# A two-layer hybrid block: the first memory columns from whole fp32 operands, reciprocal roots on GpSimd, post-norm products on VectorE, memory on ScalarE's queue

## The chip, the core and the metric

The kernel runs on one core of a Trainium2 chip. The metric is the device time of one execution in microseconds (us); lower is better. Engines are named as in the profile: PE (TensorE), PEld (its weight loads), ACT (ScalarE), DVE (VectorE), POOL (GpSimd), SP (SyncE, which issues most transfers). An "x" after a group gives its number of instructions.

## What is computed

Two layers over 256 tokens of width 1024, with a memory of 256 rows of width 1024. In each layer the normalised tokens are projected to 18 sections of 512 columns and to 5 x 1024 gate columns; five branches (stick-breaking attention, mLSTM, retention, attention to the memory, a gated MLP over tokens) are each projected up to 1024 columns, gated and summed; an out projection, a norm of its rows and the residual close the layer.

```python
def rms_norm(x, g):
    return x * lax.rsqrt(jnp.mean(x * x, axis=-1, keepdims=True) + EPS) * g

def hybrid_layer(x, mem, ...):
    proj = rms_norm(x, norm_pre) @ w_in
    ...                                             # y_sb, y_ml, y_gm, y_rt
    mkv = rms_norm(mem, mem_norm) @ w_mem_kv        # [256, 1024]: keys, values
    mem_k, mem_v = jnp.split(mkv, 2, axis=-1)
    y_xa = memory_attention(xa_q, mem_k, mem_v)
    up = einsum('bsnw,nwd->bsnd', ys, w_up)
    merged = sum(sigmoid(gates) * up, axis=2)
    return x + rms_norm(merged @ w_out, norm_post)
```

## The kernel before, in words

**Weights.** All weights stream through the core once as *halves* of 128 x 1024 fp32 (512 KB), in the order in which they are used: for each layer two chunks of memory keys (`mk`), two of memory values (`mv`), the 18 sections, gates and up projections, the out projection. A chunk is two halves. `load` (L141) issues a half's transfer on SP into one of four `raw` buffers. `split` (L155, L156) makes two fp32r tiles of it: ACT casts `whi`, DVE subtracts to get `wlo`; then it issues the load four halves on. Where a product is wanted, PE adds three fp32r matmuls, whi x hi, whi x lo and wlo x hi (L226 to L228 in `mm_proj`, L247 to L250 in `half_vproj`), the other operand being split in the same way. Plain fp32 operands are used in the branches (for example L497, L689); one such matmul shows as two records of PE.

**Order.** `step` runs one half: the split two halves on, the half's matmuls, an evacuation of PSUM, and then some units of other work from a queue. The order of instructions on each engine comes from a scheduler that works with estimated times; only SP's order, and at the very end ACT's, DVE's and POOL's too, is that of the program text.

**Start.** Five matmuls on zeros (L1102) come first. `memory` (1 MB, transposed, 8 blocks of 256 columns) and the first halves are loaded by SP in turn. `mem_split` (L329, L330) multiplies each block by the norm's gain and splits it: ACT makes `mh`, DVE makes `ml`. The first two halves give 256 memory columns (`psk`). `mem_rows` squares and sums the memory on POOL (L191 to L197), takes column sums on PE, and reciprocal roots by `rsqrt`; the rows are scaled after the projection. `x_norm_units` then norms the tokens, transposes them on PE and splits them into `hh` and `hl` (L356, L357). When the four memory chunks are through, `posb` (the positions) is loaded and `rope_tables` (L289 to L310) makes the tables of sines on DVE and ACT, ahead of the first layer.

**Reciprocal roots.** `rsqrt` is a bit trick with three Newton steps on DVE: nine small instructions for one column (L102, L103, L111, and three times L115 and L116), more for two or eight. It is used in the norms of the memory, of the tokens (`row_rsqrt`), of the branches' heads and of the gated MLP.

**End of layer 0.** The out projection leaves its result in four PSUM banks `pout`. ACT squares them (L215) and copies them to `og` (L1039), POOL multiplies by the gain (L1040); for the first 128 tokens ACT scales and POOL adds to the residual (L1048, L1049), for the others DVE does both in one (L1046). At the same time PE goes on with the memory chunks of layer 1, whose halves need ACT and DVE for `split`.

**End of layer 1.** `tail` does the same in a fixed order: products of the first 128 tokens on DVE (L1072), of the others on POOL (L1070), residuals on DVE (L1060) and once on POOL (L1083), and four output transfers.

Of the kernel before, what the change touches and what calls it, by code (L numbers as in the profile page):

```python
# [9 lines left out]
F32 = mybir.dt.float32  # L10
# [72 lines left out]
def hybrid_kernel(ctx: ExitStack, tc: tile.TileContext, x, mem, wpl, wmv, pos, vec, row, post, gmw, cst, out):  # L83
# [13 lines left out]
    def rsqrt(v, n, tag):  # L97
        """1/sqrt(v) for v > 0, [128, n]."""
        ti = tp.tile([128, n], I32, tag=tag + "i", name=tag + "i", bufs=1)
        y = tp.tile([128, n], F32, tag=tag + "y", name=tag + "y", bufs=2)  # L100
        t = tp.tile([128, n], F32, tag=tag + "t", name=tag + "t", bufs=1)
        dve.tensor_scalar(ti, v.bitcast(I32), 1, None, op0=ALU.logical_shift_right)  # L102
        dve.tensor_scalar(y[:].bitcast(I32), ti, -1.0, 1597463007.0, op0=ALU.mult, op1=ALU.add)  # L103
        if n > 2:
            for _ in range(3):
                dve.tensor_tensor(t, y, y, op=ALU.mult)
                dve.scalar_tensor_tensor(t, t, -0.5, v, op0=ALU.mult, op1=ALU.mult)
                dve.scalar_tensor_tensor(y, t, 1.5, y, op0=ALU.add, op1=ALU.mult)
            return y
        m = tp.tile([128, n], F32, tag=tag + "m", name=tag + "m", bufs=1)  # L110
        dve.tensor_scalar(m, v, -0.5, None, op0=ALU.mult)  # L111
        for _ in range(3):
            for j in range(n):
                c = slice(j, j + 1)
                dve.scalar_tensor_tensor(t[:, c], y[:, c], m[:, c], y[:, c], op0=ALU.mult, op1=ALU.mult)  # L115
            dve.scalar_tensor_tensor(y, t, 1.5, y, op0=ALU.add, op1=ALU.mult)  # L116
        return y

    # ------------------------------------------------------------------ weights
# [12 lines left out]
    def load(h, pieces=1):  # L132
        """half h of the weights; returns one transfer per piece, so that others can come between them."""
# [10 lines left out]
    def split(hi_, parts=1, between=None):  # L144
        """hi + lo = w exactly, each with a 12-bit significand."""
# [17 lines left out]
    # ------------------------------------------------------------------ constants  # L163
# [11 lines left out]
    state = {}  # L175

# [3 lines left out]
    # ------------------------------------------------------------------ norms  # L180
    def bcast_col(ps, cols):
        """cols [128 tokens, 2] (one column per token block) -> ps [128, T], the same on all partitions."""
        for tb in range(2):
            pe.transpose(ps[:, tb * 128:(tb + 1) * 128], cols(tb).to_broadcast([128, 128]), ident)

    def mem_rows():
        """1/rms of the memory rows: a column per token block, and broadcast over the partitions."""
        src = state["mem"]
        s0 = tp.tile([128, 512], F32, tag="t2", name="sq0", bufs=5)
        f = lambda i: src[:, 2 * i:2 * i + 2, :].rearrange("p a b -> p (a b)")  # L190
        pool.tensor_tensor(s0, f(0), f(0), op=ALU.mult)  # L191
        for i in range(1, 4):
            s1 = tp.tile([128, 512], F32, tag="t2", name="sq1", bufs=5)
            pool.tensor_tensor(s1, f(i), f(i), op=ALU.mult)
            pool.tensor_tensor(s0, s0, s1, op=ALU.add)
        acc = tp.tile([128, T], F32, tag="t2", name="acc", bufs=5)
        pool.tensor_tensor(acc, s0[:, 0:256], s0[:, 256:512], op=ALU.add)  # L197
# [32 lines left out]
    def half_proj(hi_, ps, xh, xl):  # L230
        """one 128-column block over all of D, into ps[:, s, :]."""
# [5 lines left out]
    def half_vproj(hi_, pss, xh, xl, n):  # L237
        """n columns, tokens on partitions, 4 of the 8 blocks of D; pss: one AP per token block."""
# [14 lines left out]
    # ------------------------------------------------------------------ work queue between weight halves  # L253
# [23 lines left out]
    def step(mm, evac=None, units=1):  # L277
        """one weight half: its matmuls, the split two halves on, the evacuation, then units of other work."""
# [8 lines left out]
    # ------------------------------------------------------------------ start  # L287
# [31 lines left out]

    def mem_split(l):  # L320
# [774 lines left out]
    with tc.manual_schedule(engines={mybir.EngineType.SP}):  # L1095
# [20 lines left out]
        for f in first[4:]:  # L1116
            f[0]()
# [110 lines left out]
```

## Time and profile before

| | |
|---|---|
| median of 3 runs | 943.66 us (942.91 to 944.35) |
| span of the profiled execution, first to last instruction | 942.9 us; no other time of this execution is recorded |
| PE busy | 922.1 us, 98% of the span, 7436 matmuls |
| DVE / ACT / POOL busy | 634.2 (67%) / 498.9 (53%) / 73.9 us (8%) |
| transfers | 165.07 MB, mean 175 GB/s |

A matmul's busy time runs from its start to its modelled end, and successive matmuls overlap, so PE's pace is read from the distance of their starts. The granted clock (PEclk) of a stretch is 1.00 at 2.4 GHz and 0.50 at 1.2 GHz.

### The profile page before, as it was taken

The numbers are of one execution on the slowest core, as the hardware profiler recorded it, in microseconds if no ns is written. First come the engines' busy times: TensorE is split into PE (matmuls) and PEld (weight loads), VectorE is DVE, ScalarE is ACT, GpSimd is POOL, SyncE is SP. The second block draws the span as 40 slices with busy tenths as digits, with TensorE's granted clock in tenths as the row PEclk, the third lists the DMA queues.
The fourth block names the chain that finished last, engine by engine and source line by source line (L and its number), as shares of the span: only waits on it lengthen the run. The fifth ranks groups of instructions, "written<-read, shape, count | busy, mean of one in ns | idle before, by whom it ended". The sixth has DMA issues, their size and how long they took to land.

```text
span 942.9 us, 18022 instructions
## 1 busy us (share of the span) xinstructions
PE 922.1 (98%) x7436; PEld 906.3 (96%) x7436; DVE 634.2 (67%) x1021; ACT 498.9 (53%) x701; POOL 73.9 (8%) x75
## 2 busy tenths in 40 slices
PE   7999999999999999999999999999999999999995
PEld 5999999999999999999889999999999999999994
DVE  6654558987785666555796444798877747755665
ACT  5664495544654544444667457754447455444452
POOL 4200010000040000000051000001000400000001
PEclk7999999999999999999999999999999999999998
DMA  7575545454455455555746554445444654555551
GB/s 257 172 251 183 181 150 165 137 189 143 155 173 193 158 171 177 182 181 188 250 146 225 196 181 157 150 164 162 157 152 152 200 181 154 165 193 184 181 188 59
DMA packets 45731, 165.07 MB, mean 175 GB/s; under 512 B 5200, under 2 KB 5328, under 8 KB 45520
## 3 DMA queue, kind: packets, MB, share of 16 engines
q1 hardware_dynamic: 45504, 163.66, 52.8%
q8 instruction: 58, 0.95, 0.4%
q10 hardware_dynamic: 144, 0.26, 0.1%
q14 instruction: 25, 0.20, 0.1%
HBM read 162.85 MB, written 1.05 MB: 174 GB/s over the span
## 4 chain that ended last, share of the span: by engine, by line
PE 94%; DVE 2%; DMA 1%; ACT 0%; issue 0%; POOL 0%; DVEq 0%; ACTq 0%
PE psp L228 19%; PE psp L227 19%; PE psp L226 19%; PE psu L227 4%; PE psu L226 4%; PE psu L228 4%; PE psp L247 3%; PE psp L250 3%; PE psp L249 3%; PE pout L1008 1%; PE pout L1006 1%; PE pout L1007 1%; PE psv L249 1%; PE psv L250 1%; PE psv L247 1%; PE pss L689 1%
## 5 line engine op out<-in xcount | busy, mean ns | idle before, releaser
L156 DVE TENSOR_TENSOR wlo<-raw,whi 128x1024 fp32r<-128x1024 f32 (+2 forms) x297 | 370.6, 1250 | 216.3 <-ACT whi L155 216.0
L155 ACT CAST whi<-raw 128x1024 fp32r<-128x1024 f32 (+2 forms) x297 | 310.3, 1047 | 358.8 <-PE psp L227 230.9
L226 PE MATMUL psp<-hh,whi 128*128 128x256 f32 x1536 | 433.6, 282 | 0.0
L227 PE MATMUL psp<-hl,whi 128*128 128x256 f32 x1536 | 433.3, 282 | 0.0
L228 PE MATMUL psp<-hh,wlo 128*128 128x256 f32 x1536 | 433.2, 282 | 0.0
L226 PEld LDWEIGHTS psp<-hh,whi 128*128 128x128 f32 x1536 | 289.5, 188 | 0.1
L227 PEld LDWEIGHTS psp<-hl,whi 128*128 128x128 f32 x1536 | 289.3, 188 | 0.1
L228 PEld LDWEIGHTS psp<-hh,wlo 128*128 128x128 f32 x1536 | 289.1, 188 | 0.2
L226 PE MATMUL psu<-yh,whi 128*128 128x256 f32 x320 | 90.3, 282 | 0.0
L227 PE MATMUL psu<-yl,whi 128*128 128x256 f32 x320 | 90.1, 282 | 0.0
L228 PE MATMUL psu<-yh,wlo 128*128 128x256 f32 x320 | 90.1, 281 | 0.0
L250 PE MATMUL psp<-whi,hl 128*128 128x256 f32 x224 | 63.1, 282 | 0.8 <-DVE hl L357 0.8
L247 PE MATMUL psp<-whi,hh 128*128 128x256 f32 x224 | 63.4, 283 | 0.0
L249 PE MATMUL psp<-wlo,hh 128*128 128x256 f32 x224 | 62.8, 281 | 0.0
L226 PEld LDWEIGHTS psu<-yh,whi 128*128 128x128 f32 x320 | 60.5, 189 | 0.0
L228 PEld LDWEIGHTS psu<-yh,wlo 128*128 128x128 f32 x320 | 60.5, 189 | 0.0
L227 PEld LDWEIGHTS psu<-yl,whi 128*128 128x128 f32 x320 | 60.3, 188 | 0.0
L250 PEld LDWEIGHTS psp<-whi,hl 128*128 128x128 f32 x224 | 42.3, 189 | 1.1 <-DVE hl L357 1.1
L247 PEld LDWEIGHTS psp<-whi,hh 128*128 128x128 f32 x224 | 42.4, 189 | 0.0
L249 PEld LDWEIGHTS psp<-wlo,hh 128*128 128x128 f32 x224 | 42.2, 188 | 0.0
L978 DVE SCALAR_TENSOR_TENSOR gate<-gate,psu 128x512 f32<-128x512 f32 x32 | 22.0, 687 | 13.0 <-PE psu L228 13.0
L1007 PE MATMUL pout<-wlo,mgh 128*128 128x512 f32 x64 | 25.2, 394 | 0.0
(294 smaller groups left out, 1086.2 us busy)
## 6 DMA issues: line engine op xcount, KB each, us to landing
raw<-in_wpl_dram SPq DMA_DIRECT2D x291, 512.0 KB, 3.7
raw<-in_wmv_dram SPq DMA_DIRECT2D x4, 528.0 KB, 4.5
rowb<-in_row_dram SPq DMA_DIRECT2D x2, 772.0 KB, 8.8
xn<-in_x_dram SPq DMA_DIRECT2D x2, 512.0 KB, 10.1
gpost<-in_post_dram SPq DMA_DIRECT2D x2, 512.0 KB, 4.8
memT<-in_mem_dram SPq DMA_DIRECT2D x1, 1024.0 KB, 4.8
cs<-in_cst_dram SPq DMA_DIRECT2D x1, 768.0 KB, 8.2
out_dram<-xn SPq DMA_DIRECT2D x3, 256.0 KB, 2.4
```

The costliest lines, as they stand in the source:

```text
L155: act.copy(hi[:, c], r[:, c])
L156: dve.tensor_tensor(lo[:, c], r[:, c], fview(hi[:, c]), op=ALU.subtract)
L226: pe.matmul(ps_ap, wh(k), xh(k), start=st, stop=False, skip_group_check=True)
L227: pe.matmul(ps_ap, wh(k), xl(k), start=False, stop=False, skip_group_check=True)
L228: pe.matmul(ps_ap, wl(k), xh(k), start=False, stop=last and k == nk - 1, skip_group_check=True)
L247: pe.matmul(ap, a, hi[:, kk * n:(kk + 1) * n], start=st and s == 0 and kk == 0, stop=False, skip_group_check=True)
L249: pe.matmul(ap, a, lo[:, kk * n:(kk + 1) * n], start=False, stop=False, skip_group_check=True)
L250: pe.matmul(ap, b, hi[:, kk * n:(kk + 1) * n], start=False, stop=s == 1 and kk == 3, skip_group_check=True)
L689: pe.matmul(ps[:, 0:256], k[:, h, 0:128], q[:, h, :], start=True, stop=False, skip_group_check=True)
L978: dve.scalar_tensor_tensor(g, g, 1.0, ps, op0=ALU.add, op1=ALU.mult)
L1006: pe.matmul(po[tb][i], a, hi[:, c], start=k == 0, stop=False)
L1007: pe.matmul(po[tb][i], a, lo[:, c], start=False, stop=False)
```

## The change

- **First memory columns.** `mem_gain` multiplies the memory by the gain on DVE into whole fp32 tiles, and `first_halves` multiplies the first two halves of the weights as loaded with these: 16 plain fp32 matmuls instead of two splits and 48 fp32r matmuls. The split memory, which the later chunks need, is still made (ACT `mh`; DVE `ml` from the product). The loads of halves 4 and 5 are issued behind these matmuls.
- **Transfers at the start.** The memory's four pieces of 256 KB are issued on ACT's queue; on SP come the gains first, then the pieces of the halves 0 and 1 in turn, halves 2 and 3, constants, tokens.
- **Sums of squares of the memory** go from POOL to ACT (squares) and DVE (three adds). The scaling of the first two `psk` banks comes after the second one.
- **Reciprocal roots.** `rsqrt` is one POOL instruction, a power with exponent -0.5, everywhere; the factor 1/D goes into the squares' scale.
- **Post norm.** In layer 0 and in `tail` the copies on ACT and products and sums on POOL are replaced: DVE multiplies PSUM by the row factor and the gain, then adds (layer 0), or multiplies and then adds with the row factor (`tail`).
- **Rope tables** are made from the queue during the projections of layer 0, behind the units that split memory keys and values.

```diff
     def rsqrt(v, n, tag):
         y = tp.tile([128, n], F32, tag=tag + "y", name=tag + "y", bufs=2)
-        dve.tensor_scalar(ti, v.bitcast(I32), 1, None, op0=ALU.logical_shift_right)
...
-            dve.scalar_tensor_tensor(y, t, 1.5, y, op0=ALU.add, op1=ALU.mult)
+        pool.tensor_tensor(y, v, mhalf[:, 0:n], op=ALU.pow)
         return y
+    def mem_squares():
+        src = state["mem"]
+        sq = [bp.tile([128, 4, T], F32, tag="z", name="msq", bufs=2) for _ in range(2)]
+        for i in range(2):
+            act.activation(sq[i], src[:, 4 * i:4 * i + 4, :], AF.Square, scale=1.0 / 32.0)
+        a, b = (t[:].rearrange("p a b -> p (a b)") for t in sq)
+        dve.tensor_tensor(a, a, b, op=ALU.add)
+        dve.tensor_tensor(a[:, 0:512], a[:, 0:512], a[:, 512:1024], op=ALU.add)
+        dve.tensor_tensor(a[:, 0:256], a[:, 0:256], a[:, 256:512], op=ALU.add)
+        state["msq"] = a
+    def first_halves(ps, xk):
+        w = [raws.pop(0), raws.pop(1)]
+        for k in range(KB):
+            for s in range(2):
+                pe.matmul(ps[:, s, :], w[s][:, k * 128:(k + 1) * 128], xk(k), start=k == 0 and s == 0,
+                          stop=k == KB - 1, skip_group_check=True)
+        count[0] = 2
+        for h in (4, 5):
+            for f in load(h):
+                f()
+    def mem_gain():
...
+        for k in range(KB):
+            dve.tensor_scalar(g[k // 4][:, k % 4, :], src[:, k, :], vcol(0, 8 + k), None, op0=ALU.mult)
+        for k in range(KB):
+            hi, lo = state["mh"][k // 4][:, k % 4, :], state["ml"][k // 4][:, k % 4, :]
+            act.activation(hi, src[:, k, :], AF.Copy, scale=vcol(0, 8 + k))
+            dve.tensor_tensor(lo, g[k // 4][:, k % 4, :], fview(hi), op=ALU.subtract)
+        return lambda k: g[k // 4][:, k % 4, :]
...
+            if l == 0 and c == 0:
+                first_halves(ps, state.pop("mg"))
+                mem_squares()
+                split(3)
+                late = [lambda ps=ps: evac(0, ps)]
+                continue
...
         queue.extend(mkv_split_units())
+        if l == 0:
+            queue.append(lambda: rope_tables(state.pop("pos")))
...
         def p1(tb):
-            og = pn[tb] = [tp.tile([128, 512], F32, tag="t2", name="og", bufs=5) for _ in range(2)]
             for i in range(2):
-                g = gpost[:, i * 512:(i + 1) * 512]
-                act.copy(og[i], po[tb][i])
-                pool.tensor_tensor(og[i], og[i], g, op=ALU.mult)
...
+                dve.scalar_tensor_tensor(og, po[tb][i], pn["r", tb], gpost[:, i * 512:(i + 1) * 512], op0=ALU.mult,
+                                         op1=ALU.mult)
+                dve.tensor_tensor(xs, xs, og, op=ALU.add)
...
                     sq = tp.tile([128, 512], F32, tag="t2", name="sq", bufs=5)
...
+                    act.activation(sq, po[tb][i], AF.Square, scale=1.0 / 32.0, accum_out=ss[:, j:j + 1])
+                    dve.tensor_tensor(og[tb][i], po[tb][i], gpost[:, c[i]], op=ALU.mult)
+                dve.scalar_tensor_tensor(v[:, tb:tb + 1], ss[:, 2 * tb:2 * tb + 1], EPS, ss[:, 2 * tb + 1:2 * tb + 2],
+                                         op0=ALU.add, op1=ALU.add)
+                r[tb] = rsqrt(v[:, tb:tb + 1], 1, f"n{tb}")
+                if tb == 0:
+                    last(0, 0, nc.sync)
+                    last(0, 1, nc.sync)
             last(1, 0, nc.scalar)
-            nc.sync.dma_start(out[:, 0, c[1]], xs(0, 1))
             last(1, 1, nc.sync)
...
+        for i in range(4):
+            nc.scalar.dma_start(state["mem"][:, 2 * i:2 * i + 2, :], mem[:, 2 * i:2 * i + 2, :])
         act.activation(warm, warm, AF.Exp)
...
         nc.sync.dma_start(vecs, vec)
...
+        for p in range(2):
+            first[0][p]()
+            first[1][p]()
         first[2][0]()
         first[3][0]()
         nc.sync.dma_start(cs[:, 0:C_RET], cst[:, 0:C_RET])
...
+        state["mg"] = mem_gain()
+        split(2)
         queue.append(mem_rows)
         queue.extend(x_norm_units(0))
-        mkv(0, [1, 0, 1, 2, 1, 1, 1, 1])
+        mkv(0, [1, 1, 2, 1, 2, 1])
```

## Rows read from the trace of the kernel before

**Rows 1.** The page's chain that ended last, shares of the span by engine.

```profile
PE 94%; DVE 2%; DMA 1%; ACT 0%; issue 0%; POOL 0%; DVEq 0%; ACTq 0%
```

**Rows 2.** Waits of PE over the span: total us, times, longest us.

```profile
PE psk L228 <- DVE wlo L156: 2.6, 2, 2.1
```

**Rows 3.** Windows at the start: busy of PE, PEld, DVE, ACT, POOL; PEclk, DMA share, GB/s.

```profile
4.00:6.00 2.00, 1.61 (x5) 1.00 (x3) 0.69 (x1) 0.56 (x1) 0.00 (x0) 1.00 0.75 162
6.00:8.00 2.00, 0.64 (x3) 0.44 (x4) 1.07 (x2) 1.10 (x3) 1.04 (x1) 1.00 1.00 363
...
20.00:22.00 2.00, 2.00 (x11) 2.00 (x11) 1.83 (x9) 1.42 (x6) 0.00 (x0) 0.50 0.80 270
```

**Rows 4.** Timeline of PE at the start: start us, us, instruction, idle before.

```profile
1.30 4.31 PE L1102 MATMUL pw<-wm 128*128 128x256 f32 x10 [1.30 <-POOL mlv L642]
...
6.95 0.38 PE L226 MATMUL psk<-mh,whi 128*128 128x256 f32 x1 [1.34 <-ACT mh L329]
...
22.95 0.27 PE L226 MATMUL psk<-mh,whi 128*128 128x256 f32 x1
```

**Rows 5.** Groups of instructions from 0 to 23 us: busy us, mean ns, idle before.

```profile
L330 DVE SCALAR_TENSOR_TENSOR ml<-memT,vecs,mh 128x256 fp32r<-128x256 f32 x8 | 9.0, 1186 | 1.7 <-ACT mh L329 1.7
...
L194 POOL TENSOR_TENSOR sq<-memT 128x512 f32<-128x512 f32 x3 | 3.9, 1321 | 1.1 <-DMA memT<-in_mem_dram 1.1
```

**Rows 6.** Timeline of PE at 117 us: two plain fp32 matmuls.

```profile
117.07 1.02 PE L497 MATMUL psz<-sb_q,sb_k 128*128 128x256 f32 x4
```

**Rows 7.** Groups over the span, forms kept apart: DVE, then POOL.

```profile
L156 DVE TENSOR_TENSOR wlo<-raw,whi 128x1024 fp32r<-128x1024 f32 x291 | 364.0, 1253 | 210.8 <-ACT whi L155 210.5
...
L811 DVE TENSOR_SCALAR xp<-xp,xs 128x256 f32<-128x256 f32 x16 | 4.9, 351 | 0.3
...
L1072 DVE TENSOR_TENSOR og<-pout,gpost 128x512 f32<-128x512 f32 x2 | 1.4, 692 | 3.2 <-ACT sq L1067 3.2
...
L873 POOL TENSOR_TENSOR gm_v<-gm_v,rowb 128x512 f32<-128x512 f32 x4 | 9.0, 2280 | 0.0
...
L197 POOL TENSOR_TENSOR acc<-sq 128x256 f32<-128x256 f32 x1 | 0.8, 795 | 0.1
```

**Rows 8.** The page's transfers of weight halves: KB each, median us to landing.

```profile
raw<-in_wpl_dram SPq DMA_DIRECT2D x291, 512.0 KB, 3.7
```

**Rows 9.** Timeline of DVE and PE from 48 to 52 us.

```profile
49.17 0.29 DVE L293 CAST pf<-posb 128x256 f32<-128x256 int32 x1 [3.36 <-DMA posb<-in_pos_dram]
...
49.91 0.39 PE L250 MATMUL psp<-whi,hl 128*128 128x256 f32 x1 [0.84 <-DVE hl L357]
...
51.74 0.39 PE L249 MATMUL psv<-wlo,hh 128*128 128x264 f32 x1 [0.60 <-DVE wlo L156]
```

**Rows 10.** Timeline of DVE and PE between the layers.

```profile
472.26 0.16 DVE L217 TENSOR_TENSOR rv<-ss 128x1 f32<-128x1 f32 x1 [1.17 <-ACT sq L215]
...
476.17 3.46 DVE L156 TENSOR_TENSOR wlo<-raw,whi 128x1024 fp32r<-128x1024 f32 x2
...
485.44 0.39 PE L228 MATMUL psk<-mh,wlo 128*128 128x256 f32 x1 [2.13 <-DVE wlo L156]
```

**Rows 11.** Windows between the layers, columns as in rows 3.

```profile
486.40:489.80 3.40, 3.40 (x19) 3.40 (x18) 3.33 (x8) 2.78 (x7) 0.79 (x1) 0.50 0.56 175
489.80:493.20 3.40, 3.40 (x30) 3.40 (x30) 3.40 (x8) 2.03 (x3) 2.05 (x2) 0.99 0.73 242
```

**Rows 12.** Timeline of the tail: DVE, ACT and SP's queue.

```profile
930.45 0.15 DVE L1078 SCALAR_TENSOR_TENSOR rv<-ss,rv 128x1 f32<-128x1 f32 x1
...
931.78 1.27 DVE L116 SCALAR_TENSOR_TENSOR n0y<-n0t,n0y 128x1 f32<-128x1 f32 x1
...
932.47 0.19 ACT L1067 ACTIVATION_READ_ACCUMULATOR sq<-pout 128x1 f32 x1
...
937.81 1.42 DVE L1060 SCALAR_TENSOR_TENSOR xn<-og,n1y,xn 128x512 f32<-128x512 f32 x2
...
939.25 0.33 SPq L1061 DMA_DIRECT2D out_dram<-xn  x1
```

More of the change, by code (lines that the diff above doesn't have):

```diff
@@ L175, in hybrid_kernel @@
     state = {}
+    mhalf = cp.tile([128, 8], F32, name="mhalf")
+    pool.memset(mhalf, -0.5)
     def vcol(l, o, n=1):
@@ L184, in bcast_col @@
             pe.transpose(ps[:, tb * 128:(tb + 1) * 128], cols(tb).to_broadcast([128, 128]), ident)
-    def mem_rows():
[L188 to L197, printed above, removed]
+    def mem_squares():
[8 more added lines that the diff above has]
+        state["msq"] = a
+    def mem_rows():
+        acc = state.pop("msq")
         ps = pz.tile([128, 512], F32, tag="sm", name="psn")
@@ L318, in mem_load @@
         nc.sync.dma_start(t, mem)
+    def mem_gain():
+        src = state["mem"]
+        g = [bp.tile([128, 4, T], F32, tag=n, name="mg", bufs=2) for n in "qk"]
+        state["mh"] = [bp.tile([128, 4, T], F32R, tag="yhi", name="mh", bufs=3) for _ in range(2)]
+        state["ml"] = [bp.tile([128, 4, T], F32R, tag="ylo", name="ml", bufs=3) for _ in range(2)]
+        for k in range(KB):
[5 more added lines that the diff above has]
+        return lambda k: g[k // 4][:, k % 4, :]
     def mem_split(l):
@@ L373, in mkv @@
                 ps = pz.tile([128, 2, T], F32, tag="sm", name="psk")
-            def evac():
-                dve.tensor_tensor(mk[2][:, 2 * c:2 * c + 2, :], ps,
-                                  rbm[:].unsqueeze(1).to_broadcast([128, 2, T]), op=ALU.mult)
-            for s in range(2):
-                step(lambda h: half_proj(h, ps, mh, ml), evac if s else None, units.pop(0))
+            if l == 0 and c == 0:
[4 more added lines that the diff above has]
+                continue
+            for s in range(2):
+                step(lambda h: half_proj(h, ps, mh, ml), (lambda: evac(c, ps)) if s and l else None, units.pop(0))
+            if l == 0:
+                for f in late:
+                    f()
+                evac(c, ps)
         for c in range(2):
@@ L1035, in p1 @@
         def p1(tb):
[L1036 removed]
             for i in range(2):
[L1038 to L1049 removed]
+                og = tp.tile([128, 512], F32, tag="t2", name="og", bufs=5)
+                xs = xn[:, tb, i * 512:(i + 1) * 512]
+                dve.scalar_tensor_tensor(og, po[tb][i], pn["r", tb], gpost[:, i * 512:(i + 1) * 512], op0=ALU.mult,
+                                         op1=ALU.mult)
+                dve.tensor_tensor(xs, xs, og, op=ALU.add)
         def tail():
@@ L1092, in layer @@
         else:
-            queue.extend([lambda f=f, tb=tb: f(tb) for tb in range(2) for f in (p0, p1, p2)])
+            queue.extend([lambda f=f, tb=tb: f(tb) for tb in range(2) for f in (p0, p1)])
     with tc.manual_schedule(engines={mybir.EngineType.SP}):
@@ L1115, in hybrid_kernel @@
         nc.sync.dma_start(cs[:, 0:C_RET], cst[:, 0:C_RET])
-        for f in first[4:]:
-            f[0]()
         for tb in range(2):
             nc.sync.dma_start(xn[:, tb, :], x[:, tb, :])
-        ms = mem_split(0)
-        split(0, 2, ms[0])
-        ms[1]()
-        ms[2]()
-        ms[3]()
-        split(1)
+        state["mg"] = mem_gain()
+        split(2)
         queue.append(mem_rows)
         queue.extend(x_norm_units(0))
-        mkv(0, [1, 0, 1, 2, 1, 1, 1, 1])
+        mkv(0, [1, 1, 2, 1, 2, 1])
         drain()
-        posb = tp.tile([128, T], I32, tag="t2", name="posb", bufs=5)
+        posb = tp.tile([128, T], I32, tag="sa", name="posb", bufs=2)
         nc.sync.dma_start(posb, pos.to_broadcast([128, T]))
         nc.sync.dma_start(cs[:, C_RET:NCST], cst[:, C_RET:NCST])
-        rope_tables(posb)
+        state["pos"] = posb
         for l in range(L):
```

62 lines of the change are left out of this document (10 added, 52 removed).

## The prediction

> **What bounds the kernel now.** I read the chain of waits first. PE holds 94% of it [rows 1]: the matmuls run back to back, so a change that leaves their number alone can only win where PE stands still, where its clock is low, or before its first and after its last useful matmul. The waits of PE name `wlo` as what it stood still for, 2.1 us at the longest [rows 2]. The timelines then put four places on the map.
>
> *Start.* PE's first memory matmul begins at 6.95, and the third half's first at 22.95 [rows 4]. In between lie 48 fp32r matmuls, which at the full clock (some 29 start in 3.4 us [rows 11], 0.12 apart) would need 5.8 us; they had 16.0. DVE's `ml` took 1186 ns each while POOL squared the memory beside it [rows 5], and the granted clock was 0.50 (1.2 GHz) as late as 20 to 22 [rows 3].
>
> *Rope tables.* DVE sits 3.36 us at `pf` until the positions land at 49.17; behind it wait the last `hl` and a `wlo`, and PE stops for 0.84 and 0.60 us [rows 9].
>
> *Between the layers.* PE stops 2.13 us for a `wlo` until 485.44 [rows 10], and in 486.40 to 489.80 the clock is 0.50 [rows 11]: 3.4 us at half pace, 1.7 us lost. Together 3.8.
>
> *Tail.* After the last matmuls DVE and POOL work alone; the last transfer is issued at 939.25 [rows 12].
>
> **The change part by part: start.** The 16 fp32 matmuls are dearer than what they replace. Two records make one; ten records of the warm-up took 4.31 us [rows 4], so 0.86 us a matmul at 1.2 GHz, and half, 0.43, at 2.4 GHz, with which four records in 1.02 us, their last end overlapping, agree [rows 6]. That is 13.8 us at the low clock or 6.9 at the full one, against 5.8 for the 48. What they save is waiting: they need the memory times the gain (8 single-source DVE instructions of 0.35 us, like L811 [rows 7]) and raw weights, no cast, no `wlo`, no `ml`, and POOL no longer squares beside DVE.
>
> When does the first one start? It needs a memory piece and a piece of each of two halves, 768 KB, where the first one before had 512 KB at 6.95 after a cast and a DVE step. One more piece is 0.7 us at the 363 GB/s of 6 to 8 us, the two steps that fall away are about as much, and the memory no longer queues behind the gains: I take 6.5. All 2.1 MB are there by about 10 us (5.8 us at 363 GB/s, and slower up to 6 us [rows 3]), before PE gets to use them at 0.86 us each, so PE is dense from 6.5. The clock came back 4.4 us after PE resumed at 485.44 [rows 10, 11]; the same here gives 10.9. By then 5.1 matmuls are done, the other 10.9 take 4.7: the end is at 15.6. Bounds: with the full clock throughout, the data bound it, the last piece at 10 and four matmuls and a gain behind it, about 12; the low clock throughout, 6.5 + 13.8 = 20.3. Against 22.95 I take 7.35.
>
> ACT's queue is the doubtful part. In 4 to 6 us one queue kept the DMA engines at a share of 0.75 and 162 GB/s, in 6 to 8 at 1.00 and 363 [rows 3], so by the row a second queue can fill at most that early stretch: if it does so fully, some 400 KB come sooner, about 1 us, and the end is 14.6. The Trainium skill (Trainium Kernel Development and Optimization, Key Constraints) says that queues of several engines run on the same 16 DMA engines and that issuing from several saves only the sequencer's issue time; by that the end stays at 15.6. The share of 1.00 with a single queue agrees. I count no gain from the queue.
>
> What is late next: halves 4 and 5. Their loads now wait for PE to finish with the raw halves, not for a split. From 15.2: issue 0.4, 3.7 to land (the median of a half [rows 8]), cast 1.05, `wlo` 1.25 [rows 7], ready near 21.6. PE has halves 2 and 3 until 15.6 + 2 x 2.8 = 21.2, and some small matmuls. I charge 1.0, between 0 and 3.7 (2 us of stall and a fall of the clock as between the layers). The split of half 2, the eight `ml`, three adds of squares (1.25 + 0.69 + 0.4) and the split of half 3 are 2.5 + 3.4 + 2.3 us on DVE and the gains 2.8: 11 us from 6.5, done by 17.5, while half 3 starts at 18.4. Covered, with 0.9 to spare. Start, net: **6.35**.
>
> **Rope tables.** In the queue they come during the `sb` projections, when the positions have long landed; about ten DVE instructions of some 0.3 us there lie under PE, with two halves split ahead. That gives back the two stops, **1.4**, with 0 as the lower bound should ACT's wait for the angles delay a cast.
>
> **The power on POOL.** The trace has none. From below: POOL's two-input products take 1.32 us at 512 columns and 0.80 at 256 [rows 5, 7], by a line through them 0.27 at one column. From above I take the longest POOL instruction, 2.28 [rows 7]. I use P = 0.8, the 256-column row: few elements, but a costlier function than a product.
>
> **Between the layers.** Leaving DVE: two Newton chains before the late `wlo` and their waits beside POOL (two `wlo` took 3.46 us instead of 2.5 [rows 7, 10]). Coming: per 128 tokens one small sum and four instructions of 0.69 [rows 7], 2.9. From the first sums at 472.26, DVE has 2 x 2.9 and three `wlo` of 1.25 to the late one: 472.3 + 5.8 + 3.75 = 481.9, plus 2P if nothing fills its waits for POOL. In-order behind that wait are the products, then `wlo`, then PE. PE ran dry at 485.44 - 2.13 = 483.3. With P = 0.8 it waits 0.2 us, too little for the clock to fall, I think: **3.6** of the 3.8. The lower bound is 0.
>
> **Tail.** The variance of the first 128 tokens is ready at 930.60, as before [rows 12]. Then P, two residuals 1.42, two products 1.38 (their squares are ready at 932.66), a sum 0.15, P, two residuals 1.42, and four handovers of about 0.1: 935.3 + 2P instead of 937.81 + 1.42 = 939.23. That is 3.95 - 2P = **2.35**; 3.4 at P = 0.27 and -0.6 at 2.28.
>
> The other roots (heads, gated MLP) lie under PE; were that cover gone, each would cost P and save about 2 us of small instructions.
>
> **Sum.** 6.35 + 1.4 + 3.6 + 2.35 = 13.7 us. The trace's span is 942.9, 0.8 below the median of the runs; against its span the sum gives 929.2, and with the 0.8 added back **930.0 us**.
>
> **Rivals.**
> 1. *The boundary still stalls.* The products come to DVE exactly where its `wlo` was late, and ahead of it in the queue. For it: the margin is 1.4 us less 2P. Against it: POOL no longer blocks DVE there. With the stop and the low clock back: 933.6.
> 2. *The start gives back.* The low clock lasts (end 20.3), or halves 4 and 5 come 2 us late and the clock falls: 2.7 to 4.7 us less, about 933.5.
> 3. *The start is better.* The clock stays at 2.4 GHz after the warm-up and the matmuls follow the data to about 12: 926.4. Against it: PE stands idle in between, and before it was at 0.50 after such a gap.
> 4. *Slow power (slower than before).* Place: two powers in a row in the tail and two between the layers, each with DVE idle behind it. In all, with the stall and the low clock back, the gain is 6.35 + 1.4 + (3.5 - 2P) + (3.95 - 2P) = 15.2 - 4P: from P = 3.8 on the kernel is slower; at P = 5 by 4.8 us, 948.5. For it: no row of this kernel shows a power. Against it: no POOL instruction exceeds 2.28. The Trainium skill (GPSIMD Engine Reference, 2.1 Instruction dispatch) says that the first call to a freshly loaded kernel pays about 6 us for code, with nothing to see in the profile; paid once, at the memory's rows, it would be hidden, since PE needs these only at the layer's start, and paid at every change between power and product the sum would be 952.3 by that figure. No run here shows it.
>
> **How the numbers follow.** Forecast 0.57 (its own range 927 to 932.5), boundary stall 0.14, start gives back 0.15, better start 0.07, slow power beyond 3.8 us 0.05, all gains spent by small stalls 0.02. The range 925.5 to 936 leaves out the slow power and the ends where several lower bounds meet. Faster by over 0.2% (about what a measurement of this kernel can tell from no change) 0.92, within 0.02, slower 0.06.
>
> **What would show it.** Right: the third half's matmuls begin near 16 instead of 22.95; two records per first matmul; no PE wait near 50 or between the layers, and no 0.50 there; the last transfer issued some 2.4 us sooner after the last matmul than before; POOL's power near 0.8. Wrong: a PE wait on `wlo` of halves 3 to 5; DVE idle behind a power for over 2 us; PE still at 0.50 beyond 13 us.

## The result and the profile after

The changed kernel takes **932.69 us** (median of 4 runs, 932.64 to 933.36) against 943.44 us for the kernel before in the same comparison: ratio 0.9887, 95% interval 0.9873 to 0.9901, 10.8 us faster. 930.0 was forecast, with a gain of 13.7. The profiled spans are 931.6 and 942.9 us, 11.3 apart; the profiled execution of the change is the slowest of its four. Lines are those of the changed kernel: `first_halves` L279, `half_proj` L213 to L215, `half_vproj` L234 to L237, `split` L139 (`whi`) and L140 (`wlo`), `mem_gain` L326 to L330, power L100, `rope_tables` L289 to L306, `tail` L1077 to L1086.

PE's share of the chain that ended last [rows 1] is now:

```profile
PE 96%; DMA 2%; DVE 1%; issue 0%; ACT 0%; SPq 0%; DVEq 0%; POOLq 0%; POOL 0%; ACTq 0%
```

PE's waits over the span answer to [rows 2]: total us, times, longest.

```profile
PE psk L279 <- DMA raw<-in_wpl_dram: 2.8, 2, 2.3
PE psv L236 <- DVE wlo L140: 2.1, 2, 1.4
```

The waits for `wlo` are no longer between the layers. PE's timeline, in order of time, with [rows 4, 9]: warm-up, first fp32 matmuls, third half, and two stops.

```profile
1.34 4.64 PE L1109 MATMUL pw<-wm 128*128 128x256 f32 x10 [1.34 <-POOL mlv L665]
8.32 0.67 PE L279 MATMUL psk<-mg,raw 128*128 128x256 f32 x2 [2.34 <-DMA raw<-in_wpl_dram]
9.47 8.43 PE L279 MATMUL psk<-mg,raw 128*128 128x256 f32 x30 [0.49 <-DMA raw<-in_wpl_dram]
17.55 0.47 PE L213 MATMUL psk<-mh,whi 128*128 128x256 f32 x1
...
26.45 0.39 PE L236 MATMUL psv<-wlo,mh 128*128 128x256 f32 x1 [0.74 <-DVE wlo L140]
...
47.09 0.39 PE L236 MATMUL psv<-wlo,hh 128*128 128x264 f32 x1 [1.38 <-DVE wlo L140]
```

**Start.** The third half begins at 17.55 instead of 22.95 [rows 4]: 5.4 us won. But the first fp32 matmul waits for weights until 8.32, PE having had nothing to do for 2.34 us, and the windows show what follows (columns as in [rows 3]; PEclk, share and GB/s come last):

```profile
4.00:6.00 2.00, 1.98 (x5) 1.01 (x3) 0.61 (x2) 1.09 (x3) 0.00 (x0) 1.00 0.89 203
6.00:8.00 2.00, 0.00 (x0) 0.00 (x0) 0.00 (x0) 0.00 (x0) 0.00 (x0) 1.00 1.01 331
8.00:10.00 2.00, 1.20 (x4) 0.73 (x5) 1.62 (x7) 1.62 (x3) 0.00 (x0) 0.89 1.06 414
10.00:12.00 2.00, 2.00 (x6) 1.65 (x5) 1.56 (x6) 1.67 (x5) 0.00 (x0) 0.50 1.01 397
12.00:14.00 2.00, 2.00 (x8) 1.63 (x8) 2.00 (x5) 2.00 (x3) 0.00 (x0) 0.75 0.97 360
```

In 6 to 8 us no engine does anything while the transfers run at a share of 1.01. The clock is at 0.50 (1.2 GHz) from about 9.6 to 13.0 (0.89 in 8 to 10, 0.75 in 12 to 14). Without POOL beside it an `ml` takes 419 ns instead of the 1186 of [rows 5]; in the kernel before, the eight `ml` of layer 1, with no POOL instruction beside them, took 480.

```profile
L330 DVE TENSOR_TENSOR ml<-mg,mh 128x256 fp32r<-128x256 f32 x8 | 2.9, 419 | 0.0
```

Half 4 makes PE stop before 26.45: 1.01 us from start to start, where two matmuls are 0.12 apart, so 0.9 lost.

**Rope tables.** They were not moved in time. DVE still stands 3.4 us in front of the positions, as in [rows 9], with a `wlo` behind them, and PE stops 1.38 us:

```profile
44.85 0.29 DVE L292 CAST pf<-posb 128x256 f32<-128x256 int32 x1 [3.38 <-DMA posb<-in_pos_dram]
45.18 0.35 DVE L293 TENSOR_SCALAR ang<-pf,cs 128x256 f32<-128x256 f32 x1
45.57 0.29 DVE L296 TENSOR_SCALAR nn<-ang 128x256 f32<-128x256 f32 x1
45.78 1.25 DVE L140 TENSOR_TENSOR wlo<-raw,whi 128x1056 fp32r<-128x1056 f32 x1
```

**Between the layers.** PE doesn't stop, and the windows that answer to [rows 11] are at 1.00:

```profile
470.00:474.00 4.00, 4.00 (x36) 4.00 (x35) 3.93 (x6) 3.16 (x7) 0.80 (x1) 1.00 0.23 71
474.00:478.00 4.00, 4.00 (x36) 4.00 (x36) 3.55 (x7) 2.51 (x5) 1.21 (x2) 1.00 0.76 247
```

From the last matmul of layer 0's out projection to the first of layer 1's sections PE took 40.28 us before (first two rows) and takes 36.25 now, 4.0 less:

```profile
473.87 0.39 PE L1008 MATMUL pout<-whi,mgl 128*128 128x512 f32 x1
514.15 0.28 PE L226 MATMUL psp<-hh,whi 128*128 128x256 f32 x1
...
468.95 0.39 PE L1033 MATMUL pout<-whi,mgl 128*128 128x512 f32 x1
505.20 0.28 PE L213 MATMUL psp<-hh,whi 128*128 128x256 f32 x1
```

The scheduler put the second power beside a `wlo`, where it took 1.64 us and made no engine on the path wait:

```profile
473.20 1.64 POOL L100 TENSOR_TENSOR n1y<-rv,mhalf 128x1 f32<-128x1 f32 x1 [5.06 <-DVE rv L205]
```

**Tail.** DVE's timeline, then one row of POOL and one of SP's queue; they answer to [rows 12]:

```profile
921.97 0.15 DVE L1086 SCALAR_TENSOR_TENSOR rv<-ss 128x1 f32<-128x1 f32 x1
922.79 1.42 DVE L1077 SCALAR_TENSOR_TENSOR xn<-og,n0y,xn 128x512 f32<-128x512 f32 x2 [0.67 <-POOL n0y L100]
924.12 1.28 DVE L1085 TENSOR_TENSOR og<-pout,gpost 128x512 f32<-128x512 f32 x2
925.32 0.15 DVE L1086 SCALAR_TENSOR_TENSOR rv<-ss 128x1 f32<-128x1 f32 x1
926.14 1.41 DVE L1077 SCALAR_TENSOR_TENSOR xn<-og,n1y,xn 128x512 f32<-128x512 f32 x2 [0.67 <-POOL n1y L100]
...
922.20 0.56 POOL L100 TENSOR_TENSOR n0y<-rv,mhalf 128x1 f32<-128x1 f32 x1 [191.96 <-DVE rv L1086]
...
927.58 0.33 SPq L1078 DMA_DIRECT2D out_dram<-xn  x1
```

From the last matmul's start (922.97) to the last issue are 4.61 us; before they were 7.76 (931.49 to 939.25): 3.15 won.

The accounting: 5.4 - 0.9 + 0.2 (the rope stop, 1.53 instead of 1.77 from start to start) + 4.0 (2.3 of stop and 1.7 of clock between the layers) + 3.15 = 11.9, against 11.3 between the spans. Most of the rest lies behind the last issue, from where the span lasts 4.1 us instead of 3.6.

### The profile page after: what moved, and what is told of

Read it like the earlier page. It is cut to its first block, busy times and chain, and to the rows that moved or that the text cites. A ratio compares the mean times of both kernels' runs of the same rounds, so it can differ in the third digit from the quotient of the medians.

```text
span 931.6 us, 17833 instructions
## 1 busy us (share of the span) xinstructions
PE 917.1 (98%) x7420; PEld 902.2 (97%) x7420; DVE 604.0 (65%) x877; ACT 494.0 (53%) x691; POOL 68.1 (7%) x74
## 4 chain that ended last, share of the span: by engine, by line
PE 96%; DMA 2%; DVE 1%; issue 0%; ACT 0%; SPq 0%; DVEq 0%; POOLq 0%; POOL 0%; ACTq 0%
PE psp L215 20%; PE psp L214 20%; PE psp L213 20%; PE psu L213 4%; PE psu L214 4%; PE psu L215 4%; PE psp L237 3%; PE psp L234 3%; PE psp L236 3%; DMA raw<-in_wpl_dram 2%; PE pout L1031 1%; PE pout L1033 1%; PE pout L1032 1%; PE psv L236 1%; PE psv L237 1%; PE psv L234 1%
## 5 line engine op out<-in xcount | busy, mean ns | idle before, releaser
L140 DVE TENSOR_TENSOR wlo<-raw,whi 128x1024 fp32r<-128x1024 f32 x294 | 365.3, 1244 | 224.6 <-ACT whi L139 223.7
L139 ACT CAST whi<-raw 128x1024 fp32r<-128x1024 f32 x294 | 308.0, 1050 | 353.1 <-PE psp L214 237.8
L213 PE MATMUL psp<-hh,whi 128*128 128x256 f32 x1536 | 433.8, 282 | 0.0
L215 PE MATMUL psp<-hh,wlo 128*128 128x256 f32 x1536 | 433.3, 282 | 0.0
L213 PEld LDWEIGHTS psp<-hh,whi 128*128 128x128 f32 x1536 | 289.5, 188 | 0.1
L215 PEld LDWEIGHTS psp<-hh,wlo 128*128 128x128 f32 x1536 | 289.2, 188 | 0.2
L213 PE MATMUL psu<-yh,whi 128*128 128x256 f32 x320 | 90.4, 282 | 0.0
L215 PE MATMUL psu<-yh,wlo 128*128 128x256 f32 x320 | 90.1, 282 | 0.0
L234 PE MATMUL psp<-whi,hh 128*128 128x256 f32 x224 | 63.1, 282 | 0.0
L237 PE MATMUL psp<-whi,hl 128*128 128x256 f32 x224 | 62.7, 280 | 0.0
L215 PEld LDWEIGHTS psu<-yh,wlo 128*128 128x128 f32 x320 | 60.5, 189 | 0.0
L213 PEld LDWEIGHTS psu<-yh,whi 128*128 128x128 f32 x320 | 60.5, 189 | 0.0
L234 PEld LDWEIGHTS psp<-whi,hh 128*128 128x128 f32 x224 | 42.4, 189 | 0.0
L237 PEld LDWEIGHTS psp<-whi,hl 128*128 128x128 f32 x224 | 42.3, 189 | 0.0
L100 POOL TENSOR_TENSOR n0y<-rv,mhalf 128x1 f32<-128x1 f32 x4 | 2.6, 649 | 402.2 <-DVE rv L205 210.3
```

The source lines that it names most:

```text
L139: act.copy(hi[:, c], r[:, c])
L140: dve.tensor_tensor(lo[:, c], r[:, c], fview(hi[:, c]), op=ALU.subtract)
L213: pe.matmul(ps_ap, wh(k), xh(k), start=st, stop=False, skip_group_check=True)
L215: pe.matmul(ps_ap, wl(k), xh(k), start=False, stop=last and k == nk - 1, skip_group_check=True)
L234: pe.matmul(ap, a, hi[:, kk * n:(kk + 1) * n], start=st and s == 0 and kk == 0, stop=False, skip_group_check=True)
L237: pe.matmul(ap, b, hi[:, kk * n:(kk + 1) * n], start=False, stop=s == 1 and kk == 3, skip_group_check=True)
```

## The experiments

All results, with ratios to the kernel before, which was timed beside each:

| run | us (range) | ratio, 95% interval |
|---|---|---|
| the change | 932.69 (932.64 to 933.36) | 0.9887, 0.9873 to 0.9901 |
| 1 Newton steps back | 939.43 (937.99 to 942.89) | 0.9957, 0.9946 to 0.9969 |
| 2 old post norm | 934.93 (934.24 to 937.13) | 0.9915, 0.9897 to 0.9934 |
| 3 old start | 937.45 (936.93 to 937.65) | 0.9935, 0.9921 to 0.9950 |
| 4 memory on SP | 931.24 (929.90 to 932.19) | 0.9869, 0.9855 to 0.9884 |
| 5 early positions | 930.95 (930.54 to 931.30) | 0.9875, 0.9860 to 0.9890 |
| 6 ten warm-up matmuls | 936.35 (935.00 to 940.14) | 0.9936, 0.9914 to 0.9958 |
| 7 halves 4, 5 early | 930.98 (930.13 to 933.14) | 0.9879, 0.9864 to 0.9894 |
| 8 = 4 + 5 | 928.66 (927.43 to 929.29) | 0.9853, 0.9837 to 0.9869 |
| 9 = 8 + later squares | 928.38 (927.78 to 929.09) | 0.9836, 0.9820 to 0.9853 |
| 10 = 5 + 6 + 7 | 931.59 (931.32 to 932.12) | 0.9870, 0.9855 to 0.9885 |
| 11 half 6 behind 4 and 5 | 932.57 (930.42 to 934.27) | 0.9878, 0.9856 to 0.9901 |
| 12 = 1 + 7 | 941.66 (938.49 to 943.00) | 0.9971, 0.9958 to 0.9984 |

The kernel before took 943.33 us beside experiments 1 to 4, 942.86 beside 5 to 8 and 943.29 beside 9 to 12, so medians of different groups compare to some 0.5 us. By the intervals 1, 3, 6 and 12 are slower than the change and 8 and 9 faster; 2, 4, 5, 7, 10 and 11 overlap with it, and what their edits do is read from the traces.

**1. The power alone undone.**

```diff
-        pool.tensor_tensor(y, v, mhalf[:, 0:n], op=ALU.pow)
+        dve.tensor_scalar(ti, v.bitcast(I32), 1, None, op0=ALU.logical_shift_right)
+        ...                      # the nine DVE instructions of before
```

> The changed kernel (932.7 us) with the bit trick and three Newton steps on DVE again in place of the power on POOL; the post norm stays on DVE. A chain undisturbed took some 1.8 us on DVE in the tail before, a power 0.56 and two handovers, so two chains in the tail cost 2 x 1.0. Theory A (the stop between the layers came from POOL's products and the residuals waiting on them, not from the chains): only the tail moves, +2.0, 934.7 us, no PE stop between the layers. Theory B (the two chains ahead of the late wlo made that stop): +2.0 and 3 to 4 us of stop and low clock, 938 us, PE waiting on wlo there.

The time is nearest theory B, the place is neither's. No `wlo` stops PE between the layers; later, where the tokens' norm for layer 1 waits on two chains, it stops three times (PE's timeline):

```profile
494.90 1.53 PE L380 MATMUL psh<-cs,xr 128*128 128x128 f32 x12 [0.33 <-DVE xr L369]
497.43 0.39 PE L249 MATMUL psp<-whi,hh 128*128 128x256 f32 x1 [1.00 <-ACT hh L384]
498.89 0.38 PE L249 MATMUL psp<-whi,hh 128*128 128x256 f32 x1 [0.55 <-ACT hh L384]
```

These stops are 1.9 us. By the starts of matmuls, the stretch from layer 0's last out projection to layer 1's first section takes 39.52 us (470.99 to 510.51) instead of 36.25, 3.3 more. The tail is 6.90 us instead of 4.61 (last issue 935.29, last matmul 928.39): 2.3, where 2.0 was expected. Of the 7.1 between the spans some 2.0 more lie at the start, where half 4 came later still (1.47 and 0.88 us of stop, then the low clock), and what follows the last issue is 0.6 shorter.

**2. The post norm alone undone.**

```diff
+                act.copy(og[i], po[tb][i])
+                pool.tensor_tensor(og[i], og[i], g, op=ALU.mult)
...
-                dve.scalar_tensor_tensor(og, po[tb][i], pn["r", tb], gpost[:, i * 512:(i + 1) * 512], op0=ALU.mult,
-                                         op1=ALU.mult)
-                dve.tensor_tensor(xs, xs, og, op=ALU.add)
```

> The changed kernel with the post norm of before in both layers (copies on ACT, products and one sum on POOL), the power kept. In the tail POOL has two products ahead of the second power, so the last issue comes some 0.8 us later. Theory A (post norm makes the stop between the layers): the stop and the low clock come back, 4 us, in all 937.5 us. Theory B (the Newton chains made it): only the tail moves, 933.5 us, no PE stop between the layers.

Nearer theory B: one stop for `xr` and no low clock (PE's timeline):

```profile
486.89 1.53 PE L365 MATMUL psh<-cs,xr 128*128 128x128 f32 x12 [0.75 <-DVE xr L354]
```

The stretch between the layers takes 37.68 us (467.74 to 505.42), 1.4 more than in the change; the tail is 5.98 us (last issue 929.17, last matmul 923.19), 1.4 longer rather than 0.8. So the 4.0 us between the layers are not the gain of one edit: undoing the power costs 3.3 there, undoing the post norm 1.4. Either one takes away the stop for `wlo`, and only both together leave no stop at all.

**3. The start alone undone.**

```diff
-        state["mg"] = mem_gain()
-        split(2)
+        ms = mem_split(0)
+        split(0, 2, ms[0])
+        ...                      # loads, squares and unit counts of before
```

> The changed kernel with the start of before: both first halves split, 48 fp32r matmuls, memory on SP's queue, squares on POOL; rope tables, powers and post norm as changed. By the accounting from the two traces the new start is worth 5.4 us at the third half's first matmul less a 0.9 us stop for halves 4 and 5: 937.2 us, the third half at 22.9, no stop near 25. If the late halves hide more of it: 935.5 us.

937.45: the new start is worth 4.8 us by the medians. In the profiles layer 0's first section starts at 55.89 instead of 51.41, 4.5 later, as the accounting says (5.4 - 0.9). The third half starts at 22.90, nothing stops PE near 25, and the stop behind the positions is 1.70.

**4. The memory on SP's queue.**

```diff
-        for i in range(4):
-            nc.scalar.dma_start(state["mem"][:, 2 * i:2 * i + 2, :], mem[:, 2 * i:2 * i + 2, :])
...
         for p in range(2):
+            nc.sync.dma_start(state["mem"][:, 4 * p:4 * p + 2, :], mem[:, 4 * p:4 * p + 2, :])
             first[0][p]()
             first[1][p]()
+            nc.sync.dma_start(state["mem"][:, 4 * p + 2:4 * p + 4, :], mem[:, 4 * p + 2:4 * p + 4, :])
```

> The changed kernel with the four pieces of the memory on SP's queue, between the pieces of the first halves (memory, half 0, half 1, memory, and so again), nothing on ACT's queue. Theory A (several queues share the same transfer engines, the second one only makes all pieces in flight together land late): the first fp32 matmul starts earlier than 8.32, near 7.2, the third half's first at 17.0 to 17.6, time 932.2 to 932.7 us. Theory B (the second queue fills the stretch up to 6 us, 207 against 162 GB/s): everything lands about 1 us later, third half at 18.5, 933.7 us.

Theory A's sign, and far more at its place than expected. PE's timeline:

```profile
5.77 0.71 PE L279 MATMUL psk<-mg,raw 128*128 128x256 f32 x2
6.84 1.56 PE L279 MATMUL psk<-mg,raw 128*128 128x256 f32 x6 [0.35 <-DMA raw<-in_wpl_dram]
9.02 5.45 PE L279 MATMUL psk<-mg,raw 128*128 128x256 f32 x24 [0.62 <-DVE mg L326]
14.12 0.47 PE L213 MATMUL psk<-mh,whi 128*128 128x256 f32 x1
...
44.50 0.39 PE L236 MATMUL psv<-wlo,hh 128*128 128x264 f32 x1 [2.10 <-DVE wlo L140]
```

The window of 4 to 6 us, on one queue:

```profile
4.00:6.00 2.00, 2.00 (x6) 1.49 (x5) 1.20 (x4) 0.91 (x2) 0.00 (x0) 1.00 0.90 280
```

The first matmul starts 2.5 us sooner, straight behind the warm-up, the clock stays at 2.4 GHz, and the third half begins 3.4 us sooner. The time falls by 1.4 us, the span by 2.5 (the change's profile is of its slowest run): no stop for half 4 is left, but the stop behind the positions grew from 1.38 to 2.10, and half 2's `wlo` makes a new one of 0.81.

**5. The positions earlier.**

```diff
             nc.sync.dma_start(xn[:, tb, :], x[:, tb, :])
+        posb = tp.tile([128, T], I32, tag="sa", name="posb", bufs=2)
+        nc.sync.dma_start(posb, pos.to_broadcast([128, T]))
...
-        posb = tp.tile([128, T], I32, tag="sa", name="posb", bufs=2)
-        nc.sync.dma_start(posb, pos.to_broadcast([128, T]))
```

> The changed kernel with the positions loaded on SP right behind the tokens, instead of after the memory's projections. Theory A (the 1.4 us stop of PE near 46 is DVE waiting for the positions, with a wlo queued behind that wait, as before the change): no wait of DVE on posb, no stop of PE there, 932.7 - 1.5 = 931.2 us, unless the early transfer delays others. Theory B (the stop is the burst of some ten table instructions on DVE itself): a stop of 1 us or more stays, 932.3 us or above.

Theory A: 1.7 us by the medians, 1.1 by the ratios (0.9875 against 0.9887). The cast that waited until 44.85 runs at 17.61, and behind its first memory matmul the profile lists no wait of PE at all.

**6. A longer warm-up.**

```diff
-        for _ in range(5):
+        for _ in range(10):
             pe.matmul(pw[:, 0:256], wm[:, 0:128], wm[:, 128:384], start=True, stop=True)
```

> The changed kernel with ten warm-up matmuls on zeros instead of five, so that PE has work until the first operands land at 8.3. Theory A (the low clock from 9.6 to 13.0 comes from PE's 2.3 us without work before the first matmul): the clock is at 2.4 GHz throughout, the 30 records from 9.47 on take 6.5 instead of 8.1 us, third half at 16.0, 931.2 us, and a little less gained if the warm-up itself runs past 8.3. Theory B (the low clock comes whatever PE did before): no change of the records' 0.427 us, and the warm-up of 8.6 us at that pace ends at 9.9: 933.5 us or more.

Theory A at its place, and 3.7 us slower in all (the profiled run took 938.57). PE's timeline, and one row of DVE:

```profile
9.21 6.74 PE L279 MATMUL psk<-mg,raw 128*128 128x256 f32 x30 [0.79 <-DMA raw<-in_wpl_dram]
15.61 0.47 PE L213 MATMUL psk<-mh,whi 128*128 128x256 f32 x1
...
24.33 0.38 PE L234 MATMUL psv<-whi,mh 128*128 128x256 f32 x1 [2.21 <-ACT whi L139]
25.59 0.52 PE L236 MATMUL psv<-wlo,mh 128*128 128x256 f32 x1 [0.88 <-DVE wlo L140]
48.23 0.39 PE L236 MATMUL psv<-wlo,hh 128*128 128x264 f32 x1 [3.61 <-DVE wlo L140]
...
46.71 0.29 DVE L292 CAST pf<-posb 128x256 f32<-128x256 int32 x1 [4.78 <-DMA posb<-in_pos_dram]
```

The third half is 1.9 us sooner. Half 4 is not: PE stops 3.1 us for it instead of 0.7, the mean clock of 20 to 30 us falls to 0.83, everything behind it is late, the positions too, and PE stops 3.6 us for these.

**7. Halves 4 and 5 early.**

```diff
-        for h in (4, 5):
-            for f in load(h):
-                f()
...
+            r = raws[h] = bp.tile([128, w], F32, tag=("yhi", "ylo")[h - 4], name="raw45", bufs=3)
```

> The changed kernel with halves 4 and 5 loaded into two buffers that are free at the start, issued behind the tokens, so that their loads don't wait for the fp32 matmuls. Theory A (the 0.9 us stop at 25.4 is the late arrival of these halves): it is gone, 931.8 us. Theory B (something else of the start, the order of ACT and DVE, holds them): the stop stays, 932.7 us. Against both, 1 MB more in flight early could make the first pieces later: 933 us or more.

Theory A at its place: no stop at 25. The time is not decided: 1.7 us less by the medians, 0.8 by the ratios, and in the profile, which is of the slowest of the four runs, the last matmul starts at 923.23, no sooner than in the change (922.97). There the third half began 0.7 later (18.25, the clock being at 0.50 from 8 to 14), and two stops behind the positions remain, 1.32 and 0.54.

**8. Memory on SP and early positions**, edits 4 and 5 together.

> Two edits together on the changed kernel: the memory's pieces on SP's queue among those of the first halves (931.2 us alone) and the positions loaded behind the tokens. With the memory on SP the stop of PE for the wlo behind the positions grew to 2.1 us (from 1.4), so theory A (that stop is the positions' wait) gives 931.2 - 2.1 = 929.1 us with no stop near 45; theory B (the start's gain is paid back later by whatever waits next, for example ACT's casts or late halves) gives 930.5 us or more, with a new stop between 15 and 60.

928.66, theory A. The third half starts at 13.86, and no stop is left behind the one of 0.96 at 15.3.

**9. The squares of the memory later.** To 8 this adds, with one more unit of the queue in the first step:

```diff
-                mem_squares()
                 split(3)
...
+        queue.append(mem_squares)
         queue.append(mem_rows)
```

> The version with the memory on SP and early positions (928.7 us) with a third edit: the squares of the memory and their adds are taken from the queue behind the split of half 3, so that DVE's first add no longer stands ahead of the wlo of half 2, for which PE stops 0.96 us at 15.3. Theory A (that add is what makes the wlo late): no stop at 15.3, 927.7 us. Theory B (the wlo waits for its data or its cast, not for the add): the stop stays, 928.7 us.

Not decided: the scheduler left the add where it was (DVE, 13.14, ahead of the `wlo` at 14.29), and PE stopped 0.82 us at 15.6, and now 0.58 at 24.0. 928.38 us is the lowest median here, within the spread of 8.

**10. Longer warm-up with edits 5 and 7.**

> The changed kernel with three edits: ten warm-up matmuls, halves 4 and 5 into free buffers at the start, positions behind the tokens. Ten warm-up matmuls alone made it slower (936.3) although the third half began 1.9 us sooner. Theory A (what they gained was lost in the stops for half 4 and for the positions, 3.1 and 3.6 us, and the low clock behind each): without those stops the third half is at 15.6, nothing stops PE at 25 or 47, and the time is 932.7 - 1.9 - 0.9 - 1.5 = 928.4 us. Theory B (the longer warm-up costs by itself): 931 us or more, although no stop for halves 4 and 5 or the positions is left.

Half of each. The two stops that theory A blamed are gone, and 4.8 us with them (936.35 to 931.59). But PE now gets to half 2 before DVE has split it, and the clock falls (PE's timeline, then windows):

```profile
18.08 0.38 PE L218 MATMUL psk<-mh,wlo 128*128 128x256 f32 x1 [0.86 <-DVE wlo L143]
```

```profile
18.00:20.00 2.00, 1.92 (x13) 1.92 (x14) 1.26 (x4) 2.00 (x8) 0.55 (x1) 0.84 0.71 259
20.00:22.00 2.00, 2.00 (x12) 2.00 (x11) 1.39 (x4) 0.82 (x2) 1.13 (x2) 0.50 0.70 211
22.00:24.00 2.00, 2.00 (x16) 2.00 (x16) 1.93 (x5) 1.39 (x2) 0.26 (x1) 0.81 0.91 303
```

The lost pace is (0.16 + 0.50 + 0.19) x 2 = 1.7 us.

**11. Half 6 behind halves 4 and 5 on SP's queue.**

```diff
+        if hi_ == 2:
+            return
         for f in load(hi_ + NRAW) or ():
...
-        for h in (4, 5):
+        for h in (4, 5, 6):
```

> The changed kernel with only the order of three loads on SP's queue changed: half 6 is issued behind halves 4 and 5, not ahead of them. Theory A (half 4 lands 6.6 us after its issue, not 3.7, because half 6's 512 KB go ahead of it): half 4 lands near 21.5, its wlo is ready before 24.5, no stop at 25.4, 931.8 us. Theory B (half 4 is late because its buffer waits for the fp32 matmuls until 17.3): it lands as late as before, 932.7 us. If half 6 comes too late instead: a stop near 31.

Half 4 is cast at 19.97 instead of 24.09, and PE doesn't stop there. But the edit changed more than the order. SP's queue, half 4 in the change and here:

```profile
17.50 0.33 SPq L125 DMA_DIRECT2D raw<-in_wpl_dram  x1
...
16.08 0.33 SPq L125 DMA_DIRECT2D raw<-in_wpl_dram  x1
```

It was issued 1.4 us sooner, as soon as DVE had split half 2, without the wait for the fp32 matmuls, and it landed 3.9 us after its issue instead of 6.6. So of the 4.1 us, 2.7 go with theory A's cause and 1.4 with theory B's. The time is unclear (four runs, 930.42, 931.06, 934.09 and 934.27; the profile is of the third): in the profile the stop behind the positions is 1.90, and the clock falls after it (0.80 in 45 to 50).

**12. Newton steps with halves 4 and 5 early.**

> The version with Newton steps on DVE again (939.4 us), and halves 4 and 5 into free buffers at the start. In that version PE stopped 1.5 and 0.9 us near 25 and then ran at the low clock from 26.5 to 29.4. Theory A (that is the late half 4, a stop that was on the edge of a fall of the clock, not the power's doing): 2.35 and some 1.4 us come back, 935.7 us, and the power by itself is worth what is left above the version with halves 4 and 5 early (931.0), 4.7 us: 2.3 in the tail, 1.9 between the layers. Theory B (the chain of the memory's roots on DVE makes it late): the stop stays, 939 us.

The stop at 25 is gone, as theory A says, but the time isn't: PE comes to the positions sooner and stops 2.89 us at 43.97, and 0.34, 1.00 and 0.56 us at 492.88 to 496.88, as in 1. The profile is of the fastest run (938.49, mean granted clock 0.994); the five runs of 942 to 943 us had 0.989 to 0.991, and where their clock was low is not recorded, so the median prices nothing. The profile prices the power by place, beside 7, from which it differs by the power alone: 39.53 us between the layers instead of 36.25, and 6.90 in the tail instead of 4.61, 5.6 together. At the start the two profiles differ in the clock too, so what the power is worth there stays open.

## Why the prediction was right, and where it was not

**Direction and most of the size: right.** The time lies in the range, 0.2 above the forecast's own (927 to 932.5). The total is better than its terms: the start and the rope tables gave about 3 us less than forecast, the layers and the tail 1.2 more.

**Start, forecast 6.35 net, measured 4.5** (experiment 3: 4.8 in time). The step that failed is the arrival of the first operands, 6.5 forecast, 8.32 measured; the last of the first 2.1 MB landed at 11.6, 10 forecast. What followed came out in number: the clock was back 4.7 us after the first matmul (near 13.0), 4.4 were taken, and the end moved by as much as the beginning (1.95 and 1.8). In mechanism it differed: PE was not dense from its first matmul, which ran before the clock fell, but stood 0.49 us in front of the next, and the low clock began only near 9.6.

I had priced the second queue between nothing and 1 us gained, and had left out the loss. By 2.3 us both queues had 1.8 MB under way, four memory pieces and three of weights. A weight piece issued at 1.25 landed at about 8.3, and so did the second memory piece, issued at 1.24 on the other queue. With one queue (experiment 4) pieces land in the order of need, the first two of the weights at 5.42 and 6.79 instead of 8.18 and 9.43. More bytes did not help: in the first 8 us two queues moved 189 GB/s and one 177 (in 4 to 6 us 203 and 280). The Trainium skill (DMA: Bandwidth & Descriptors, Queues, rings and completion order) says that each transfer engine takes packets from its queues in turn; the trace agrees: the first matmul's weights landed together with memory that was not needed yet. Here rival 3 (the clock stays, the end near 12, 926.4) was to be had: experiment 4 reached 14.12. It changes the queue and the order of issue at once, so which of the two does it is not shown.

**Halves 4 and 5, charged 1.0, measured 0.9.** The number is right by luck: the load waited for PE, as forecast, but landed 6.6 us after its issue instead of 3.7, with half 6 ahead of it on SP's queue (experiment 11); and PE came to half 4 7.7 us after the start of half 2 instead of 5.6, for the small matmuls that the sum names without a price. With 3.7 us to land, `wlo` would have been ready near 23.6, before PE wanted it. One of the prediction's signs of being wrong, a wait on the `wlo` of halves 3 to 5, came.

**Rope tables, forecast 1.4, measured 0.2.** The step "in the queue they come during the `sb` projections" failed. The queue sets the text's order, and the scheduler sets DVE's; presumably the positions had landed by its estimate, which no run shows. I gave the lower bound of 0 for another reason, a late cast. Experiment 5 gets the gain (1.1 to 1.7) by moving the load.

This stop has a second effect, which the forecast lacked: it takes back part of what is won ahead of it. PE waits there for a transfer that moves with the start too, but by less: PE came 3.3, 0.7 and 4.6 us sooner in experiments 4, 11 and 12 than in the change, the positions only 2.6, 0.2 and 2.4, and the stop of 1.38 us became 2.10, 1.90 and 2.89. In 6 PE came 1.1 sooner and the positions 1.9 later: 3.61. With the stop gone (8) experiment 4's gain shows.

**Between the layers, forecast 3.6, measured 4.0.** Right in size. That the chains and the POOL products were each enough to make PE wait (3.3 and 1.4 us, experiments 1 and 2) was not forecast.

**Tail, forecast 2.35, measured 3.15.** The mis-sized term is P: 0.8 taken, 0.56 measured, which makes the formula 2.83. The remaining 0.3 is covered by the rows of the tail: the four handovers took 0.22 instead of 0.4, the two products 1.28 instead of 1.38, and neighbours on DVE overlap by 0.09 and 0.08.

**Slow power: no.** The 16 powers took 0.55 to 1.65 us. The Trainium skill (GPSIMD Engine Reference, 2.1 Instruction dispatch) has about 6 us for the first call to a freshly loaded kernel; no run here shows it, the first power of the profile took 0.55 at 18.03 and DVE went on 0.7 us after its sum.

The best version is the change with experiments 4 and 5 (928.7; with 9 it is 928.4, within the spread).

## What to carry to other kernels

At a start, the order in which bytes land counts as much as how many are under way: here it paid to issue what the first matmul needs, in that order on one queue, with nothing beside it. Before a gain at the start is counted, look for the next wait whose end moves less than the start does (here the positions, and the half that stood behind another in the queue), because such a wait takes back part of the gain, and with a fall of the clock all of it and more (experiment 6). Where a scheduler orders the engines, moving an instruction in the text is a request; moving the load it waits for is what changed the time.

## What the runs showed of the hardware

The column of the granted clock can miss the low level at the start. In experiment 5 it says 1.00 from 8 to 14 us, while a record of the first fp32 matmuls takes 652 ns, and 379 from 15 on (one of its windows; groups of 9 to 14 and of 15 to 18 us):

```profile
10.00:12.00 2.00, 2.00 (x6) 1.55 (x6) 1.62 (x6) 1.78 (x6) 0.00 (x0) 1.00 1.01 390
...
L279 PE MATMUL psk<-mg,raw 128*128 128x256 f32 x13 | 6.0, 652 | 2.3 <-DMA raw<-in_wpl_dram 2.3
...
L279 PE MATMUL psk<-mg,raw 128*128 128x256 f32 x15 | 3.4, 379 | 0.0
```

The warm-up's records too took 650 ns at a shown 1.00. The Trainium skill (TensorE: Matmul & The Clock Gate, Part 1) warns of the clock's records; this trace agrees, and the length of equal matmuls is the better clock.

Whether a stop of PE was followed by 0.50 differed, and the length of the stop alone does not tell: after 0.86 us at 18.08 in experiment 10, 1.90 in 11 and 2.13 in the kernel before it was; after 0.74 and 1.38 in the change, 0.96 at 15.3 in 8, 2.10 in 4 and 2.89 in 12 it was not, and there the matmuls behind the stop start 0.12 us apart, as at 2.4 GHz.

A power on one column took 0.56 us alone, and 1.64 in the one case in which it started beside a `wlo` of two SBUF operands. DVE shows the same on the other side: an `ml` of the kernel before took 480 ns alone and 1186 on the average beside POOL's squares.
